# First attention of an encoder trunk: each turn of probabilities set directly ahead of later scores, dense steps dealt out anew

## Chip, cores and metric

One core of a Trainium2 chip runs the whole kernel in one launch. The metric is the device time of that launch in microseconds (us); a run's time is compared with runs of the kernel before. A difference of under 0.2% (2.7 us of 1348.9) can't be told from none.

## What is computed

Two layers on a sequence of 512 tokens of 1024 features, all in float32: layer 0 is windowed grouped-query attention with a sink logit, layer 1 a dilated attention in three groups, and each is followed by a SwiGLU block. The change touches layer 0's attention alone:

```python
def window_gqa_sink(h, w_qkv, w_out, sink):
    qkv = h @ w_qkv          # 16 query heads, 4 key/value heads of 64
    o, lse = banded_attention(q, k, v, slopes, 1, WINDOW_A, BLOCK_A)   # |t-s| <= 128, blocks of 128 queries
    o = o * jax.nn.sigmoid(lse - sink)
    return o.reshape(b, s, H_A * HEAD_DIM) @ w_out
```

In `banded_attention` the scores q·k get a bias from the distance, the probabilities are `exp(scores - max)` divided by their sum, and they weigh the values.

## The kernel before, in words

**Dense products.** The float32 operands of a dense product are split into a high and a low part (`split`, L115 on ScalarE for the high part `wh`, L116 on VectorE for the low part `wl`), and three matmuls stand for one product (`mm3`, L144). A dense product of 128 output features for all 512 tokens is a *unit* of 8 steps; a step is 6 matmuls of 256 columns. Weights arrive by DMA in buffers of three, and the two splits of a unit are made when a generator of that unit is first asked for a step.

**Attention in pieces.** Layer 0's attention is cut into 16 attention units (key-head pair P, half h, query block b; the list `units`). Unit n has four heads, and these steps:

- two score steps, `scores(0)` and `scores(1)`, numbered 2n and 2n+1 here (scores 0 to 31). Each is four matmuls (L168) into two PSUM banks with the tag `sc`, of which there are two. On the outer blocks (b = 0 and 3) they have 256 columns, on the inner ones 384. What follows each, on other engines: VectorE adds the bias and takes the maximum of both banks (L436, one instruction for each bank, *the reduction*), makes the negative maximum (L440), ScalarE takes the exponential of each (L443), VectorE the reciprocal (L445), and GpSimd scales (L447, tile `pr`).
- two or three turns (L454): four TensorE transposes of a 128-wide stretch of `pr` into a bank with the tag `tp`, of which there are two, then a copy out to `pt`, on VectorE for the second stretch (L458), else on ScalarE (L460). Turns are numbered 0 to 39 through the program. A turn needs `pr` of all four heads, so the scaling behind both score steps.
- a share in one of four weighings (L467): `weigh_four` takes four units at once, 40 matmuls; it writes one bank `sc` and the bank `ov`, and ScalarE and VectorE split the outcome (`oh` L484, `ol` L485).

**Order.** TensorE's order is the program's own. VectorE, ScalarE, GpSimd and SyncE get theirs from the scheduler, and each then runs its queue strictly in turn. In the program, units run two ahead: between the turns of unit n stand the score steps of unit n+2, and *dense steps* of another list (`fill`: the rest of the values' product, queries and keys of the second head pairs, the first parts of the output product) fill the time in which VectorE, ScalarE and GpSimd work. How many dense steps unit n gets is `counts[n]`; `weave` divides them evenly over the entries of its list of steps. Before unit 0 the number of dense steps between the first score steps is in the call of `spread`. These are L529 to L543 of the main body. In all 86 dense steps are spent here.

So what TensorE can wait for in this stretch is: a bank `sc` that a reduction (L436) has not yet read, for scores and for a weighing; `pr` that GpSimd has not yet scaled, for a turn; a bank `tp` whose copy isn't done.

Of the kernel before, what the change touches and what calls it, by code (L numbers as in the profile page):

```python
# [79 lines left out]
def trunk(ctx, tc, xT, gains, lastg, sink, tabs, qsc, wunits, wv, outT, outR):  # L80
# [96 lines left out]
    def chain(*gens):  # L177
        for _, g in gens:
            yield from g

    def weave(main, fill, total):

        done = 0
        for i, step in enumerate(main):
            want = total * (i + 1) // len(main)
            spread([step, want - done], fill)
            done = want

    def spread(main, fill):

        for step in main:
            if callable(step):
                step()
            else:
                for _ in range(step):
                    next(fill)
# [173 lines left out]
    with tc.tile_pool(name="l0", bufs=2) as pool:  # L370
# [10 lines left out]
        def late(gen):  # L381
            for _ in gen:
                for item in list(pending):
                    item[0] -= 1
                    if item[0] < 0:
                        pending.remove(item)
                        item[1]()
                yield

        def k_unit(P, **kw):  # L390
            def done(ps):
                t = spool.tile([128, S], F32, name="tmp")
                nc.vector.tensor_tensor(t, ps, norm["rb"], op=OP.mult)
                qk["k", P] = [pool.tile([128, S], F32R, name=f"kt{a}") for a in range(2)]
                qk["kl", P] = [pool.tile([128, S], F32R, name=f"kl{a}") for a in range(2)]
                split_keys(t, qk["k", P], qk["kl", P])
            return unit(5 * P, xh, xl, "mm", done, **kw)

        def q_unit(P, i, **kw):
            def done(ps):  # L400
                t = spool.tile([128, S], F32, name="tmp")
                col = 4 * P + i
                nc.vector.scalar_tensor_tensor(t, ps, qs_sb[:, col:col + 1], norm["rb"], op0=OP.mult, op1=OP.mult)
                qk["q", P, i] = apart(pool, any(k[0] == "q" for k in qk), lambda: [
                    pool.tile([128, S], F32R, name=f"qt{a}", bufs=6) for a in range(2)])
                if col < 2:
                    split_queries(t, qk["q", P, i])
                else:
                    pending.append([2, lambda: split_queries(t, qk["q", P, i])])
            return unit(5 * P + 1 + i, xh, xl, "mm", done, **kw)  # L410
# [63 lines left out]
        def weigh_four(n):  # L474

            for m, tag in ((n, "sc"), (n + 2, "ov")):
                ov = bank(tag, "ov")
                for k in range(2):
                    units[m + k][2](ov, k)
                P, h, b = m // 8, m // 4 % 2, m % 4  # L480
                own = slice(4 * P + 2 * h, 4 * P + 2 * h + 2)
                hi, lo = (t[:, own, 128 * b:128 * b + 256].rearrange("p i (b q) -> p b i q", b=2) for t in (oh, ol))
                src = ov.rearrange("p (b i q) -> p b i q", b=2, i=2)
                nc.scalar.activation(hi, src, AF.Copy)  # L484
                nc.vector.tensor_tensor(lo, src, hi.bitcast(F32), op=OP.subtract)  # L485
# [21 lines left out]
        def out_part(j, lo, hi, w={}, ahead=False):  # L507
            def gen():
                if lo == 0:
                    w[j] = load_unit(wunits[10 + j], (NK, 128))  # L510
                    if ahead:
                        yield
                    out_ps[j] = bank("mm")
                wh, wl = w[j]
                for c in range(lo, hi):
                    mm3(out_ps[j], wh[:, c], wl[:, c], oh[:, c, :], ol[:, c, :], c == 0, c == NK - 1)
                    if c == NK - 1:
                        residual(j, out_ps[j], 1)
                    yield
            return hi - lo, gen()  # L520
# [4 lines left out]
        fill = late(chain((16, early), q_unit(0, 2), q_unit(0, 3), k_unit(1),  # L525
                     *[q_unit(1, i) for i in range(4)],
                     *[out_part(j, 0, 4) for j in range(3)], *[out_part(j, 4, 6) for j in range(3)]))

        counts = [6, 7, 6, 5, 5, 5, 4, 4, 4, 4, 3, 2, 2, 2, 3, 2]  # L529
        units = [attention0(P, h, b) for P in range(2) for h in range(2) for b in range(4)]  # L530
        (s0, s1), (s2, s3) = units[0][0], units[1][0]
        spread([13, s0, 2, s1, 2, s2, 2, s3, 3], fill)
        for n, (_, rest, _) in enumerate(units):
            nexts = units[n + 2][0] if n + 2 < len(units) else []
            steps = []
            for k in range(len(rest)):
                steps += rest[k:k + 1]
                if k == 0 and n and n % 4 == 0:
                    steps.append(lambda: weigh_four(n - 4))
                steps += nexts[k:k + 1]  # L540
            if n == len(units) - 1:
                steps.append(lambda: weigh_four(n - 3))
            weave(steps, fill, counts[n])  # L543
# [588 lines left out]
    with tc.tile_pool(name="l1", bufs=2) as pool:  # L1132
# [41 lines left out]
        def behind(step):  # L1174
            def held():
                with tc.issue_after(newest(mybir.EngineType.Activation)):
                    step()
            return held
# [482 lines left out]
        def attention(p):  # L1661


            pts = {}

            def turn(ts):
                for t in ts:
                    pts[t] = turn_a(p, ts, t)

            def weigh():  # L1670
                early = p % 2 == 0 and p > 0
                if early:
                    scores_b(p, (0, 1))
                    scores_b(p, (2, 3))
                if p:
                    finish(p - 1)
                for t in range(4):
                    weigh_a(p, t, pts[t])
                if not early:
                    scores_b(p, (0, 1))  # L1680
                    scores_b(p, (2, 3))

            def turn_back():
                for cs in ((0, 1), (2, 3)):
                    st["pts", p, cs[0]] = turn_b(p, cs)
                merge_rows(p)

            low, high = (0, 1), (2, 3)
            return {"a01": lambda: scores_a(p, low), "a23": lambda: scores_a(p, high), "merge": lambda: merge(p),
                    "xa01": lambda: st["exps", p, low, "a"](), "xa23": lambda: st["exps", p, high, "a"](),  # L1690
                    "t01": lambda: turn(low), "t23": lambda: turn(high), "group": weigh,
                    "x0": lambda: st["exps", p, low](0), "x1": lambda: st["exps", p, low](1),
                    "x2": lambda: st["exps", p, high](2), "x3": lambda: st["exps", p, high](3),
                    "r01": lambda: st["rest", p, low](), "r23": lambda: st["rest", p, high](), "back": turn_back}
# [27 lines left out]
        def lined(made):  # L1722

            line, work = [], {}
            for n, gen, preps in made:
                for at, step in preps:
                    work.setdefault(max(len(line) + at, 0), []).append(step)
                line += [gen] * n
            for c, gen in enumerate(line):
                for step in work.pop(c, ()):  # L1730
                    step()
                next(gen, None)
                yield
# [31 lines left out]
        for _ in range(2):  # L1765
            both = pool.tile([128, 4, 256], F32, name="v1", bufs=3).rearrange("p (a b) f -> p a (b f)", a=2)
# [26 lines left out]
        counts = [sum(unit[0] for unit in units) for units in periods]  # L1793
        out_line = [plain_unit(j, lo, hi) for lo, hi in ((0, 6), (6, 7)) for j in range(3)]
        fill = lined([unit for units in periods for unit in units] + out_line)
# [28 lines left out]
        for p in range(8):  # L1824
# [6 lines left out]
            steps = attention(p)  # L1831
            steps = {name: behind(step) if f"{name}{p % 2}" in BEHIND else step for name, step in steps.items()}
# [98 lines left out]
```

## Time and profile before

| what | value |
|---|---|
| median of 3 runs | 1348.9 us (1347.6 to 1349.86) |
| the profiled execution's own time | 1346.77 us |
| its span | 1345.0 us |
| TensorE busy in the span | 1329.5 us (99%) |
| VectorE, ScalarE, GpSimd busy | 1071.2, 812.8, 286.0 us |
| granted TensorE clock | 1.00 |
| VectorE busy in 36 to 150 us | 80.08 of 114.00 us |
| ScalarE busy in 36 to 150 us | 76.72 of 114.00 us |

The first attention fills about 38 to 150 us of the span. In a row of the timeline stand the start, the duration, the engine, the line, the operation, out<-in, the shape and the count; behind it, in square brackets, how long the engine was idle before it and what ended that. Matmuls overlap one another, so a matmul's duration is not its cost: the cost is the distance from its start to the start of the next.

### The profile page before, as it was taken

What the parts mean: (1) busy time and instruction counts of PE and PEld (TensorE: products, weight loads), DVE (VectorE), ACT (ScalarE), POOL (GpSimd) and SP (SyncE); (2) the same over time, 40 slices, a digit from 0 to 9 for tenths busy, and PEclk for the clock granted to TensorE, in tenths of its full rate; (3) what the DMA queues carried; (4) which work ended last, traced back from release to release, by engine and by line L of the source; (5) the groups of instructions that cost most, each with busy time, mean ns of one, the idle gap of its engine ahead of it and who ended that gap; (6) DMA issues with size and microseconds to landing.
All of it is one profiled execution on the core that took longest, in us unless ns stands there. A gap on an engine that the chain in (4) does not pass through costs nothing.

```text
span 1345.0 us, 29672 instructions
## 1 busy us (share of the span) xinstructions
PE 1329.5 (99%) x11874; PEld 1309.5 (97%) x11874; DVE 1071.2 (80%) x1911; ACT 812.8 (60%) x1480; POOL 286.0 (21%) x388
## 2 busy tenths in 40 slices
PE   9999999999999999999999999999999999999998
PEld 8988999999999999999999999999999999999998
DVE  6776648877779999888888888888566887878995
ACT  6776534555555467667777667667454455555643
POOL 1233330111111001123314314313131011110203
PEclk9999999999999999999999999999999999999999
DMA  6210262688775547285556656655346388784822
GB/s 211 64 54 27 66 179 95 167 210 192 193 171 144 157 145 203 72 215 135 153 143 164 154 140 163 155 140 142 111 127 164 107 209 204 187 197 122 202 85 75
DMA packets 89914, 196.49 MB, mean 146 GB/s; under 512 B 11184, under 2 KB 17840, under 8 KB 89776
## 3 DMA queue, kind: packets, MB, share of 16 engines
q1 hardware_dynamic: 67072, 153.82, 36.2%
q0 software_dynamic: 22560, 40.52, 18.3%
q8 instruction: 93, 1.52, 0.5%
q14 instruction: 45, 0.37, 0.1%
q10 hardware_dynamic: 144, 0.26, 0.1%
HBM read 188.72 MB, written 5.84 MB: 145 GB/s over the span
## 4 chain that ended last, share of the span: by engine, by line
PE 85%; ACT 6%; DVE 4%; issue 2%; DMA 1%; SPq 0%; POOL 0%; DVEq 0%; ACTq 0%; POOLq 0%
PE mm L781 19%; PE sc L781 14%; PE mm L1337 13%; PE mm L144 12%; PE psv L144 9%; PE tp L144 6%; PE sc L144 2%; PE ov L467 1%; PE ov L144 1%; ACT pr L1587 1%; PE sc L1501 1%; ACT pr L443 1%; DVE wl L116 1%; PE ovb L1627 1%; PE tp L1529 1%
## 5 line engine op out<-in xcount | busy, mean ns | idle before, releaser
L737 POOL DMA_DIRECT2D w<-wunits x92 | 80.5, 916 | 446.5 <-DMA w<-wunits 187.6
L116 DVE TENSOR_TENSOR wl<-wraw,wh 128x1024 fp32r<-128x1024 f32 (+4 forms) x92 | 98.0, 1075 | 17.3 <-ACT wh L115 14.8
L115 ACT ACTIVATE wh<-wraw 128x1024 fp32r<-128x1024 f32 (+4 forms) x91 | 83.0, 928 | 45.2 <-PE mm L144 38.7
L781 PE MATMUL sc<-bh,wh 128*128 128x256 f32 x368 | 101.6, 276 | 0.0
L781 PE MATMUL mm<-bh,wl 128*128 128x256 f32 x368 | 101.6, 276 | 0.0
L781 PE MATMUL mm<-bh,h 128*128 128x256 f32 x368 | 101.6, 276 | 0.0
L781 PE MATMUL mm<-bh,wh 128*128 128x256 f32 x368 | 101.6, 276 | 0.0
L781 PE MATMUL sc<-bh,wl 128*128 128x256 f32 x368 | 101.6, 276 | 0.0
L781 PE MATMUL mm<-bl,wh 128*128 128x256 f32 x368 | 101.6, 276 | 0.0
L781 PE MATMUL sc<-bl,wh 128*128 128x256 f32 x368 | 101.6, 276 | 0.0
L781 PE MATMUL mm<-bl,h 128*128 128x256 f32 x368 | 101.6, 276 | 0.0
L781 PE MATMUL mm<-bh,l 128*128 128x256 f32 x368 | 101.6, 276 | 0.0
L144 PE MATMUL mm<-xh,wh 128*128 128x256 f32 x384 | 77.8, 284 | 0.0
L1337 PE MATMUL mm<-oh,slots 128*128 128x256 f32 x368 | 73.8, 285 | 2.4 <-ACT ssum L1352 2.0
L144 PE MATMUL mm<-xl,wh 128*128 128x256 f32 x384 | 75.5, 278 | 0.3 <-DVE xl L281 0.3
L144 PE MATMUL mm<-xh,wl 128*128 128x256 f32 x384 | 75.5, 278 | 0.2 <-DVE wl L116 0.2
L144 PE MATMUL psv<-wh,oh 128*128 128x256 f32 x256 | 71.2, 278 | 0.0
L144 PE MATMUL psv<-wl,oh 128*128 128x256 f32 x256 | 71.0, 277 | 0.2 <-DVE wl L116 0.2
L144 PE MATMUL psv<-wh,ol 128*128 128x256 f32 x256 | 70.9, 277 | 0.0
L781 PEld LDWEIGHTS mm<-bh,wh 128*128 128x128 f32 x368 | 69.1, 188 | 0.0
L781 PEld LDWEIGHTS sc<-bl,wh 128*128 128x128 f32 x368 | 69.1, 188 | 0.0
L781 PEld LDWEIGHTS mm<-bl,h 128*128 128x128 f32 x368 | 69.1, 188 | 0.0
(361 smaller groups left out, 5134.9 us busy)
## 6 DMA issues: line engine op xcount, KB each, us to landing
wraw<-wunits SPq DMA_DIRECT2D x118, 512.0 KB, 4.2
w<-wunits SPq DMA_DIRECT2D x207, 256.0 KB, 3.9
w<-wunits POOLq DMA_DIRECT2D x138, 256.0 KB, 6.3
wraw<-wv SPq DMA_DIRECT2D x21, 512.0 KB, 5.0
wraw<-wunits SPq DMA_DIRECT2D x16, 384.0 KB, 5.0
w<-wv SPq DMA_DIRECT2D x8, 512.0 KB, 4.3
w<-wv POOLq DMA_DIRECT2D x8, 512.0 KB, 7.3
wraw<-wunits SPq DMA_DIRECT2D x11, 256.0 KB, 3.2
```

Source lines behind the costliest of these rows:

```text
L115: nc.scalar.activation(out_h, src, AF.Copy)
L116: nc.vector.tensor_tensor(out_l, src, out_h.bitcast(F32), op=OP.subtract)
L144: nc.tensor.matmul(out[:, cols], a, b[:, cols], start=first and k == 0 and c == 0, stop=last and k == 2, skip_group_check=True)
L443: nc.scalar.activation(pr[:, e, :w + 1], pr[:, e, :w + 1], AF.Exp, bias=m[:, 1, e:e + 1], accum_out=m[:, 2, e:e + 1])
L467: nc.tensor.matmul(ov[64 * hf:64 * hf + 64, 256 * n:256 * n + 256], v0[:, k0 // 128 + kb, vs], st["pt", kb][:, 256 * hf:256 * hf + 256], s ...
L737: nc.gpsimd.dma_start(sums[:, 512 * k:512 * k + 512], v[:, 0:512], accum_op=OP.add)
L781: nc.tensor.matmul(out, a[:, j], b[:, j], start=first and j == 0 and i == 0, stop=j == 3 and i == 2, skip_group_check=True)
L1337: nc.tensor.matmul(out, a[:, j], b[:, j], start=first and j == 0 and i == 0, stop=j == 3 and i == 2, skip_group_check=True)
L1501: nc.tensor.matmul(out, qk["qs", p][a][:, 128 * t:128 * t + 128], kp[k], start=t == ts[0] and k == 0, stop=k == 1, skip_group_check=True)
L1529: nc.tensor.transpose(tp[:, (nb * a + kb) * 128:(nb * a + kb) * 128 + 128], st["pr", p, ts][:, a, o + 128 * kb:o + 128 * kb + 128], ident)
L1587: nc.scalar.activation(of(pr[:, a, :], c), of(pr[:, a, :], c), AF.Exp, bias=nm[:, c % 2, a:a + 1], accum_out=den[:, c % 2, a:a + 1])
L1627: nc.tensor.matmul(ov[rows, 128 * c:128 * c + 128], vals[p // 2, 1 + g][:, c, hv + 64 * a:hv + 64 * a + 64], pts[g][:, 256 * a + 128 * (c ...
```

## The change

Two things change, both in layer 0's attention. In the list of steps of unit n, the first turn and the first score step of unit n+2 become one entry, and so do the second turn and the second score step: no dense step stands between a turn and those scores any longer. Where a weighing belongs to unit n (n = 4, 8, 12), it now comes ahead of that unit's first turn, as an entry of its own. And the numbers of dense steps are others: `counts`, and the numbers between the first score steps. The total of dense steps stays 86.

```diff
-        counts = [6, 7, 6, 5, 5, 5, 4, 4, 4, 4, 3, 2, 2, 2, 3, 2]
+        counts = [6, 7, 6, 6, 4, 5, 3, 4, 4, 5, 1, 2, 2, 3, 3, 2]
         units = [attention0(P, h, b) for P in range(2) for h in range(2) for b in range(4)]
         (s0, s1), (s2, s3) = units[0][0], units[1][0]
-        spread([13, s0, 2, s1, 2, s2, 2, s3, 3], fill)
+        spread([13, s0, 2, s1, 1, s2, 4, s3, 3], fill)
         for n, (_, rest, _) in enumerate(units):
             nexts = units[n + 2][0] if n + 2 < len(units) else []
             steps = []
             for k in range(len(rest)):
-                steps += rest[k:k + 1]
+                both = rest[k:k + 1] if k else rest[:1] + nexts[:1]
                 if k == 0 and n and n % 4 == 0:
                     steps.append(lambda: weigh_four(n - 4))
-                steps += nexts[k:k + 1]
+                if k == 1:
+                    both = both + nexts[1:2]
+                steps.append(lambda both=both: [step() for step in both])
             if n == len(units) - 1:
                 steps.append(lambda: weigh_four(n - 3))
             weave(steps, fill, counts[n])
```

Three places show it. First TensorE around the second weighing. Before: scores 19 (four matmuls), one dense step, turn 20, the weighing, the next dense step.

```order
L168 MATMUL sc<-kt_873,qt_1176 128x384
L168 MATMUL sc<-kl_875,qt_1176 128x384
L168 MATMUL sc<-kt_874,qt_1177 128x384
L168 MATMUL sc<-kl_876,qt_1177 128x384
L144 MATMUL mm<-xh,wh 128x256 x2
L144 MATMUL mm<-xl,wh 128x256 x2
L144 MATMUL mm<-xh,wl 128x256 x2
L454 MATMUL tp<-ident,pr 128x128 x4
L467 MATMUL ov<-pt,v_101 64x256 x20
```

Of the change, the same place: turn 19, scores 19, two dense steps, the weighing.

```order
L454 MATMUL tp<-ident,pr 128x128 x4
L168 MATMUL sc<-kt_866,qt_1169 128x384
L168 MATMUL sc<-kl_868,qt_1169 128x384
L168 MATMUL sc<-kt_867,qt_1170 128x384
L168 MATMUL sc<-kl_869,qt_1170 128x384
L144 MATMUL mm<-xh,wh 128x256 x2
L144 MATMUL mm<-xl,wh 128x256 x2
L144 MATMUL mm<-xh,wl 128x256 x2
L144 MATMUL mm<-xh,wh 128x256 x2
L144 MATMUL mm<-xl,wh 128x256 x2
L144 MATMUL mm<-xh,wl 128x256 x2
L467 MATMUL ov<-pt,v_101 64x256 x20
```

Turn 20 has moved behind the weighing, and a second dense step stands between scores 19 and the weighing.

Second, VectorE at that place. Before: the reciprocal of scores 17, the split of a weight (L116), the two reductions of scores 18, the two parts of a split of queries (L155) around the negative maximum, the copy of turn 19, the first reduction of scores 19.

```order
L445 RECIPROCAL mst<-mst 128x2
L116 TENSOR_TENSOR wl<-wraw,wh 128x1024
L436 ISA pr,mst<-sc,tab_102 128x384
L436 ISA mst 128x1
L436 ISA pr,mst<-sc,tab_102 128x384
L436 ISA mst 128x1
L155 TENSOR_TENSOR qt_1338<-tmp,qt_1338 64x512
L440 SCALAR_TENSOR_TENSOR mst<-mst,nsink 128x2
L155 TENSOR_TENSOR qt_1339<-tmp,qt_1339 64x512
L458 COPY pt<-tp 128x512
L436 ISA pr,mst<-sc,tab_102 128x384
```

Of the change: the second reduction of scores 18, the same query splits and copy, both reductions of scores 19, the reciprocal of scores 18, and only then the split of the weight.

```order
L436 ISA pr,mst<-sc,tab_102 128x384
L436 ISA mst 128x1
L155 TENSOR_TENSOR qt_1338<-tmp,qt_1338 64x512
L440 SCALAR_TENSOR_TENSOR mst<-mst,nsink 128x2
L155 TENSOR_TENSOR qt_1339<-tmp,qt_1339 64x512
L458 COPY pt<-tp 128x512
L436 ISA pr,mst<-sc,tab_102 128x384
L436 ISA mst 128x1
L436 ISA pr,mst<-sc,tab_102 128x384
L436 ISA mst 128x1
L445 RECIPROCAL mst<-mst 128x2
L116 TENSOR_TENSOR wl<-wraw,wh 128x1024
```

The split of the weight has gone from ahead of scores 18 to behind scores 19.

Third, TensorE at unit 10. Before: scores 24, a dense step, turn 26, scores 25.

```order
L168 MATMUL sc<-kt_873,qt_1338 128x256
L168 MATMUL sc<-kl_875,qt_1338 128x256
L168 MATMUL sc<-kt_874,qt_1339 128x256
L168 MATMUL sc<-kl_876,qt_1339 128x256
L144 MATMUL mm<-oh,wh 128x256 x2
L144 MATMUL mm<-ol,wh 128x256 x2
L144 MATMUL mm<-oh,wl 128x256 x2
L454 MATMUL tp<-ident,pr 128x128 x4
L168 MATMUL sc<-kt_873,qt_1519 128x256
```

Of the change, from turn 25 to turn 27, with no dense step in it:

```order
L454 MATMUL tp<-ident,pr 128x128 x4
L168 MATMUL sc<-kt_866,qt_1338 128x256
L168 MATMUL sc<-kl_868,qt_1338 128x256
L168 MATMUL sc<-kt_867,qt_1339 128x256
L168 MATMUL sc<-kl_869,qt_1339 128x256
L454 MATMUL tp<-ident,pr 128x128 x4
L168 MATMUL sc<-kt_866,qt_1519 128x256
L168 MATMUL sc<-kl_868,qt_1519 128x256
L168 MATMUL sc<-kt_867,qt_1520 128x256
L168 MATMUL sc<-kl_869,qt_1520 128x256
L454 MATMUL tp<-ident,pr 128x128 x4
```

Between scores 24 and 25 only turn 26 is left. The four engines' instructions are the same in number and kind before and after, SyncE's order is the same, and outside the first attention no engine's order differs.

## The prediction

> **What bounds the kernel now.** I read the page first, then busy time by stretches, the waits of the first attention (36 to 150 us), and last the timeline of TensorE and VectorE there. The page:
>
> ```profile
> span 1345.0 us, 29672 instructions
> PE 1329.5 (99%) x11874; PEld 1309.5 (97%) x11874; DVE 1071.2 (80%) x1911; ACT 812.8 (60%) x1480; POOL 286.0 (21%) x388
> ```
>
> TensorE is busy nearly all the span, so only time that it loses can be won. Busy time by stretches, where the count of matmuls is in brackets:
>
> ```profile
> 100.00:125.00 25.00, 23.67 (x193) 21.43 (x193) 18.59 (x62) 16.29 (x44) 10.33 (x24) 1.00 0.14 43
> 225.00:250.00 25.00, 25.00 (x223) 25.00 (x222) 19.34 (x23) 12.80 (x17) 0.00 (x0) 1.00 0.35 107
> ```
>
> Within the first attention TensorE idles a little (23.67 of 25 us); in the dense block behind it, it doesn't. Both run at the full clock, 1.00. The waits there name the cause:
>
> ```profile
> PEld sc L168 <- DVE mst L436: 3.0, 8, 1.0
> ```
>
> Scores wait eight times for a reduction that has not yet read their bank. VectorE isn't out of capacity (18.59 of 25 us busy); its queue is at times in a bad order. To size each loss I need what a thing costs undisturbed. Scores 18, a dense step; then turn 15 with scores 16 directly behind it; then turn 30 with a weighing:
>
> ```profile
> 96.05 0.33 PE L168 MATMUL sc<-kt,qt 128*128 128x384 f32 x1
> ...
> 96.74 0.39 PE L144 MATMUL mm<-xh,wh 128*128 128x256 f32 x2
> ...
> 97.43 0.60 PE L454 MATMUL tp<-ident,pr 128*128 128x128 f32 x4
> ...
> 89.92 0.60 PE L454 MATMUL tp<-ident,pr 128*128 128x128 f32 x4
> 90.28 0.37 PE L168 MATMUL sc<-kt,qt 128*128 128x256 f32 x1
> ...
> 90.83 0.39 PE L144 MATMUL mm<-xh,wh 128*128 128x256 f32 x2
> ...
> 125.71 0.60 PE L454 MATMUL tp<-ident,pr 128*128 128x128 f32 x4
> 126.24 0.44 PE L467 MATMUL ov<-pt,v 128*64 128x256 f32 x2
> ```
>
> From start to start: scores of 384 columns 96.74 - 96.05 = 0.69, a dense step 97.43 - 96.74 = 0.69 (its thirds 0.23), a turn 0.36, a turn and scores of 256 together 90.83 - 89.92 = 0.91, a turn ahead of a weighing 0.53. Scores of 256 take two thirds of 0.69, 0.46. A turn directly ahead of scores thus costs TensorE nothing by itself (0.91 against 0.36 + 0.46 and the 0.09 that whatever follows a turn pays). The pairing is neutral; what counts is when banks come free.
>
> **What it removes.** The places where TensorE loses time, in order: ahead of and in scores 9, scores 11, scores 19, the second weighing, scores 24, scores 29, turn 35.
>
> ```profile
> 63.83 0.39 PE L144 MATMUL mm<-xh,wl 128*128 128x256 f32 x2
> 64.32 0.38 PE L168 MATMUL sc<-kt,qt 128*128 128x256 f32 x1
> ...
> 65.01 0.40 PE L144 MATMUL mm<-xh,wh 128*128 128x256 f32 x2
> ...
> 70.95 0.39 PE L144 MATMUL mm<-xh,wl 128*128 128x256 f32 x2
> 71.43 0.44 PE L168 MATMUL sc<-kt,qt 128*128 128x384 f32 x1
> ...
> 72.36 0.28 PE L144 MATMUL mm<-xh,wh 128*128 128x256 f32 x1
> ...
> 98.35 0.39 PE L144 MATMUL mm<-xh,wl 128*128 128x256 f32 x2
> 99.55 0.45 PE L168 MATMUL sc<-kt,qt 128*128 128x384 f32 x1 [0.81 <-DVE mst L436]
> ...
> 100.48 0.39 PE L144 MATMUL mm<-xh,wh 128*128 128x256 f32 x2
> ...
> 101.17 0.60 PE L454 MATMUL tp<-ident,pr 128*128 128x128 f32 x4
> 102.85 0.44 PE L467 MATMUL ov<-pt,v 128*64 128x256 f32 x2 [1.08 <-DVE mst L436]
> ...
> 117.01 0.60 PE L454 MATMUL tp<-ident,pr 128*128 128x128 f32 x4
> ...
> 118.55 0.28 PE L144 MATMUL mm<-oh,wh 128*128 128x256 f32 x1
> ...
> 132.19 0.60 PE L454 MATMUL tp<-ident,pr 128*128 128x128 f32 x4
> ...
> 133.61 0.39 PE L144 MATMUL mm<-oh,wh 128*128 128x256 f32 x2
> ...
> 137.94 1.16 PE L454 MATMUL tp<-ident,pr 128*128 128x128 f32 x4
> 138.85 0.36 PE L144 MATMUL mm<-oh,wh 128*128 128x256 f32 x1
> ```
>
> - Scores 9: due at 63.83 + 0.23 = 64.06, begun at 64.32 (0.26); then 0.69 long where 256 columns take 0.46 (0.23). Scores that had to wait run slower by about 0.23 besides. Together 0.49.
> - Scores 11: due at 71.18, begun at 71.43 (0.25), 0.93 instead of 0.69 (0.24): 0.49.
> - Scores 19: due at 98.58, begun at 99.55 (0.97), and 0.93 instead of 0.69 (0.24): 1.21.
> - Second weighing: 102.85 - 101.17 = 1.68 against 0.53: 1.15.
> - Turn 25 and scores 24: 118.55 - 117.01 = 1.54 against 0.91: 0.63.
> - Turn 31 and scores 29: 133.61 - 132.19 = 1.42 against 0.91 + 0.23 for the wider scores: 0.28.
> - Turn 35: 138.85 - 137.94 = 0.91 against 0.36: 0.55, a wait for GpSimd's scaling.
>
> The sum is 4.80 us, the most that the change can win; what scores 1 lose, below, stays, since both orders begin alike. Why the largest two go, VectorE shows:
>
> ```profile
> 97.79 1.23 DVE L116 TENSOR_TENSOR wl<-wraw,wh 128x1024 fp32r<-128x1024 f32 x1 [1.26 <-ACT wh L115]
> 98.94 0.55 DVE L436 CUSTOM_DVE_ANT_0 pr<-sc,tab 128x384 f32<-128x384 f32 x1
> ...
> 102.23 0.56 DVE L436 CUSTOM_DVE_ANT_0 pr<-sc,tab 128x384 f32<-128x384 f32 x1
> ```
>
> Scores 18 are done about 96.7, but in VectorE's queue a weight split stands ahead of their reduction; it idles 1.26 us for ScalarE's part and then works 1.23, so the reduction begins at 98.94. That delays scores 19 by 0.97, and the reduction of scores 19, at 102.23, delays the weighing. In the changed order the split stands behind both reductions of scores 19. Nothing else in that queue waits for ScalarE that long, and two dense steps instead of one and a turn stand ahead of the weighing. The others go by spacing, counted in the changed order: between scores 7 and 8 stand five dense steps instead of four (the reductions of 8, for which scores 9 waited, come up earlier beside them), between 10 and 11 three instead of two, between 23 and 24 four instead of two; scores 29 no longer meet the output split of the third weighing (L485) in front of their bank, since turn 30 now follows that weighing; and by turn 35 the reductions have caught up by some 0.6 us. I walked every score step, turn and weighing of the changed order through in this manner, each engine's queue in its order with the durations of before. All seven come out at zero. The margins are 0.1 to 0.7 us, so not each will.
>
> **What it adds.** Ahead of scores 2 stands one dense step where there were two:
>
> ```profile
> 40.25 0.38 PE L168 MATMUL sc<-kt,qt 128*128 128x256 f32 x1
> ...
> 41.66 0.42 DVE L436 CUSTOM_DVE_ANT_0 pr<-sc,tab 128x256 f32<-128x256 f32 x1
> ```
>
> Scores 1, begun at 40.25 late and slowed as scores 9 are (0.69), end at 40.94; a dense step later, at 41.63, scores 2 are due. The first bank is read from 41.66 to 42.08, in a part of VectorE's queue that is the same in both orders, so they begin at about 42.13: 0.50 lost, and 0.24 for the slow run, 0.74. This is the surest term. The dense step that is missing there follows later; it is moved, not spared.
>
> Scores 25 follow scores 24 with turn 26 alone between: due 0.46 + 0.36 = 0.82 us behind their start. From below it costs nothing, if VectorE is idle when scores 24 end; from above it costs 1.21, as scores 19 did. VectorE isn't idle: ahead of that reduction stand a query split and the reciprocal of scores 23, which waits for ScalarE. Nearest is scores 24 of before, which lost 0.63 with the same query splits ahead; I take 0.70.
>
> The second weighing: by my walk the reduction that frees its bank ends just when the weighing is due, 99.6 us on the clock of before. So it costs between zero and the 1.15 of today. What can shift it is a slowed query split:
>
> ```profile
> 90.26 1.40 DVE L116 TENSOR_TENSOR wl<-wraw,wh 128x1024 fp32r<-128x1024 f32 x1
> ...
> 90.11 1.90 POOL L447 TENSOR_SCALAR pr<-pr,mst 128x256 f32<-128x256 f32 x2 [0.28 <-DVE mst L445]
> L447 POOL TENSOR_SCALAR pr<-pr,mst 128x256 f32<-128x256 f32 x32 | 15.9, 509 | 37.4 <-DVE mst L440 25.6 <-DVE mst L445 11.6
> ```
>
> Two scalings that met a weight split took 1.90 us instead of twice 0.51, and the split 1.40 instead of 1.23: 0.17 for VectorE. In the changed order GpSimd's scaling of scores 17 falls on the two query splits ahead of that reduction: 2 x 0.17, so I take 0.35. [...]
>
> No instruction is added or taken away, no DMA issue moves in its queue, and dense steps only change places: cost zero, hidden by nothing, since TensorE does the same work. What ScalarE and GpSimd do later or earlier stays beside TensorE as long as no bank is missed. Behind 150 us TensorE was full and stays so; what it wins is handed through to the end, as the weights there are asked for in the same order when their buffers come free.
>
> **The sum.** 0.74 + 0.70 + 0.35 - 4.80 = -3.0 us. The profiled execution took 1346.77 us with a span of 1345.0, so it becomes 1343.8 and 1342.0. It lay 2.1 us under the median of the runs shown, 1348.9; carried over, the forecast is 1345.9. Of what a measurement can tell, 0.2% or 2.7 us, this is just beyond.
>
> **Rivals.**
> - *Tight places slip.* Several margins are 0.1 to 0.3 us (the second and third weighing, scores 5, 17 and 31). Each one missed costs its lateness and the 0.24 of slowed scores, some 0.5. With three missed, 3 x 0.5 = 1.5 is left of the gain: 1347.4. For it speaks that VectorE's durations vary by 0.2 (1.23 and 1.40 above); against it, that its idle time in the stretch is a quarter.
> - *Slower: narrowed pairs wait for a VectorE queue.* At six places (scores 12 and 13, 14 and 15, 16 and 17, 20 and 21, 22 and 23, 24 and 25) two dense steps and a turn, or two dense steps, between a pair's scores have shrunk by one. Of 384-column scores the bank of the first is read about 1.2 us after their start (0.63 until the first two matmuls have ended and VectorE has begun, an estimate from 96.05 and 0.33, then 0.55) and wanted after 0.69 + 0.69 + 0.36 = 1.74. From 0.55 us of delay in the queue each pair waits. If a weight split or its like stands ahead at each, as at scores 19, six times 1.21 is lost, and 7.3 + 0.7 - 4.8 = +3.2: 1352.1. For it speaks scores 25; against it that in the changed order of VectorE only copies of turns and a scaling of queries stand there, and no weight split directly ahead of any of these reductions but those of scores 18 in the order before.
> - *It does nothing for the end.* What TensorE wins here it waits later, for weights of the next block: 1348.9. The windows speak against it: 223 matmuls in 25 us behind the attention, with the DMA engines busy a third (0.35).
>
> **How the numbers follow.** My forecast gets 0.55, tight places 0.35, slower 0.05, nothing 0.05. Likeliest is 1345.9. From above the gain is bounded by 4.80 - 0.74 = 4.1 with both unknown costs at zero, 1344.8; the runs spread by about 1 us around their median, so the low end is 1344.0. The other end takes in the slipped places, 1347.4, and the same 1 us: 1348.4. Faster by over 0.2% is under 1346.2, which is my forecast but not the slipped places: 0.55. Within 0.2% are those and the case that nothing comes of it: 0.40. Slower: 0.05.
>
> **What would show it.** The last weighing of before begins here:
>
> ```profile
> 143.62 0.65 PE L467 MATMUL ov<-pt,v 128*64 128x256 f32 x4
> ```
>
> In the changed profile: scores 19 and the second weighing without an idle time for a reduction; the weight split (L116) there behind the reductions; scores 2 begun about 0.5 us after they are due, scores 25 with a wait of some 0.5; the first attention's last weighing about 3 us earlier than 143.62, and every later stretch as full as before. I am wrong if scores 12 to 23 show new waits for L436, if turns wait for GpSimd (L447) in more than one place, or if the last weighing is early and the end isn't.

## The result, and the profile after

The changed kernel took 1344.76 us (median of 7 runs, 1341.92 to 1346.2), the kernel before 1347.6 beside it (7 runs): a ratio of 0.9976, 95% interval 0.9965 to 0.9986. It is faster by 0.24%, 3.2 us, with 1.9 to 4.7 inside the interval. One execution of a kernel below (new entries in units 6 to 8 only) took 4736.83 us and is left out of its ratio. The profiled execution of the change took 1343.19 us, before 1346.77. Its page:

```profile
span 1341.4 us, 29671 instructions
PE 1328.7 (99%) x11874; PEld 1311.3 (98%) x11874; DVE 1071.1 (80%) x1911; ACT 813.3 (61%) x1480; POOL 287.1 (21%) x388
```

The work is the same on every engine to within about 1 us (VectorE 1071.1 against 1071.2, GpSimd 287.1 against 286.0); the span is 3.6 shorter. The waits of the first attention, 36 to 150 us, with the time in total, the number and the longest (PEld is TensorE's loading of weights, which stands ahead of the matmul):

```profile
PEld sc L168 <- DVE mst L436: 1.3, 3, 0.6
PEld ov L467 <- DVE mst L436: 0.2, 1, 0.2
```

The second weighing's wait of before, in the same view:

```profile
PEld ov L467 <- DVE mst L436: 1.3, 1, 1.3
```

Eight waits of scores have become three (scores 1, 2 and 25), the second weighing's load waits 0.2 where it had waited 1.3, and no turn waits for GpSimd. By stretches, TensorE gains in the attention, and stands as full behind it as it did. In such a row stand the stretch and its length, the busy time and number of instructions of TensorE, its weight loads, VectorE, ScalarE and GpSimd, the granted clock, the DMA engines' busy share and GB/s:

```profile
100.00:125.00 25.00, 24.85 (x208) 21.99 (x206) 17.78 (x62) 17.66 (x48) 12.73 (x28) 1.00 0.13 43
225.00:250.00 25.00, 25.00 (x223) 25.00 (x223) 20.44 (x24) 12.96 (x17) 1.77 (x2) 1.00 0.37 115
```

208 matmuls stand where 193 stood, though not all of them the same ones, since the program is some 3 us further on. TensorE's timeline at the places of the prediction: scores 0 and 2; turn 19 with scores 19 and the second weighing; turns 25 to 27 around scores 24 and 25; the last weighing.

```profile
37.39 0.28 PE L168 MATMUL sc<-kt,qt 128*128 128x256 f32 x1
...
40.62 0.39 PE L144 MATMUL mm<-xh,wl 128*128 128x256 f32 x2
41.37 0.45 PE L168 MATMUL sc<-kt,qt 128*128 128x384 f32 x1 [0.36 <-DVE mst L436]
...
42.17 0.40 PE L144 MATMUL mm<-xh,wh 128*128 128x256 f32 x2
...
96.36 0.60 PE L454 MATMUL tp<-ident,pr 128*128 128x128 f32 x4
96.72 0.42 PE L168 MATMUL sc<-kt,qt 128*128 128x384 f32 x1
...
98.69 0.40 PE L144 MATMUL mm<-xh,wl 128*128 128x256 f32 x2
99.08 4.54 PE L467 MATMUL ov<-pt,v 128*64 128x256 f32 x40
...
114.45 0.60 PE L454 MATMUL tp<-ident,pr 128*128 128x128 f32 x4
...
115.36 0.60 PE L454 MATMUL tp<-ident,pr 128*128 128x128 f32 x4
116.12 0.39 PE L168 MATMUL sc<-kt,qt 128*128 128x256 f32 x1 [0.15 <-DVE mst L436]
...
116.81 0.60 PE L454 MATMUL tp<-ident,pr 128*128 128x128 f32 x4
...
139.16 0.40 PE L144 MATMUL mm<-oh,wl 128*128 128x256 f32 x2
139.49 4.54 PE L467 MATMUL ov<-pt,v 128*64 128x256 f32 x40
```

Scores 19 begin 0.36 behind their turn, as undisturbed ones do. Scores 2 are due at 40.62 + 0.23 = 40.85, begin at 41.37 and run 0.80 instead of 0.69: 0.63 lost. Turn 26 with scores 25 takes 116.81 - 115.36 = 1.45, turn 25 with scores 24 115.36 - 114.45 = 0.91: 0.54 lost. The second weighing begins 99.08 - 98.69 = 0.39 behind the last third of a dense step, the last weighing 0.33: 0.06 lost. VectorE there:

```profile
97.12 0.71 DVE L155 TENSOR_TENSOR qt<-tmp,qt 64x512 fp32r<-64x512 f32 x1
...
98.46 0.56 DVE L436 CUSTOM_DVE_ANT_0 pr<-sc,tab 128x384 f32<-128x384 f32 x1
...
98.94 0.55 DVE L436 CUSTOM_DVE_ANT_0 pr<-sc,tab 128x384 f32<-128x384 f32 x1
...
99.50 1.20 DVE L116 TENSOR_TENSOR wl<-wraw,wh 128x1024 fp32r<-128x1024 f32 x1
```

The weight split follows both reductions of scores 19, and its 1.26 of waiting for ScalarE is gone too. The reduction that frees the weighing's bank ends at 98.46 + 0.56 = 99.02, the moment at which the weighing is due.

The size of the gain is best read from the start of scores 0 to the start of the last weighing. For that, the start of scores 0 before (its last weighing began at 143.62):

```profile
38.19 0.28 PE L168 MATMUL sc<-kt,qt 128*128 128x256 f32 x1
```

Before 143.62 - 38.19 = 105.43 us, after 139.49 - 37.39 = 102.10: 3.33 less. This *stretch* is used below for every kernel; it leaves out the start of the program, which was 0.80 shorter in this execution, and what follows.

### The profile page after: what moved, and what is told of

The parts are those of the page before. It is cut to its first block, busy times and chain, and to the rows that moved or that the text cites. A ratio compares the mean times of both kernels' runs of the same rounds, so it can differ in the third digit from the quotient of the medians.

```text
span 1341.4 us, 29671 instructions
## 1 busy us (share of the span) xinstructions
PE 1328.7 (99%) x11874; PEld 1311.3 (98%) x11874; DVE 1071.1 (80%) x1911; ACT 813.3 (61%) x1480; POOL 287.1 (21%) x388
## 4 chain that ended last, share of the span: by engine, by line
PE 90%; ACT 4%; DVE 4%; issue 1%; DVEq 0%; POOL 0%; ACTq 0%; POOLq 0%
PE mm L783 18%; PE mm L144 15%; PE mm L1339 14%; PE sc L783 14%; PE psv L144 9%; PE tp L144 6%; PE sc L144 2%; PE ov L467 1%; PE ov L144 1%; PE sc L168 1%; PE ovb L1629 1%; PE tp L454 1%; PE sc L1503 1%; ACT pr L1589 1%; PE sc L1569 1%
## 5 line engine op out<-in xcount | busy, mean ns | idle before, releaser
L116 DVE TENSOR_TENSOR wl<-wraw,wh 128x1024 fp32r<-128x1024 f32 (+4 forms) x92 | 98.7, 1082 | 15.7 <-ACT wh L115 13.1
L783 PEld LDWEIGHTS mm<-bh,l 128*128 128x128 f32 x368 | 69.1, 188 | 0.0
```

Of the source, the lines that this page charges most:

```text
L116: nc.vector.tensor_tensor(out_l, src, out_h.bitcast(F32), op=OP.subtract)
L783: nc.tensor.matmul(out, a[:, j], b[:, j], start=first and j == 0 and i == 0, stop=j == 3 and i == 2, skip_group_check=True)
```

## The experiments

My theory, A: TensorE loses time only where a reduction comes too late for its bank; the new entries set the turns and scores, the new numbers of dense steps give each bank its time, and it takes both. Rivals: the new entries alone do it (B), the new numbers alone (C); later, that one place in the middle carries nearly all (D), that the weight split is not the cause at scores 19 (F), and that a wait removed in one place turns up at another (E). The summary, with the ratio to the kernel before (95% interval) and the stretch of the profiled execution:

| kernel | ratio | stretch, us |
|---|---|---|
| before | 1 | 105.43 |
| the change | 0.9976 (0.9965 to 0.9986) | 102.10 |
| new entries only | 0.9993 (0.9985 to 1.0002) | 104.42 |
| new numbers only | 1.0002 (0.9993 to 1.0011) | 105.85 |
| new entries in units 6 to 8 only | 0.9982 (0.9973 to 0.9991) | 104.31 |
| the change without these | 0.9976 (0.9967 to 0.9986) | 101.85 |
| before, one weight split on GpSimd | 1.0006 (0.9997 to 1.0015) | 107.24 |
| the change, a step more ahead of scores 2 | 0.9971 (0.9961 to 0.9981) | 102.19 |
| the change, room at scores 25 | 0.9964 (0.9952 to 0.9977) | 102.15 |
| both of these | 0.9967 (0.9954 to 0.9979) | 101.93 |
| the change again | 0.9973 (0.9964 to 0.9982) | 102.41 |
| the change, unit 14 with two steps | 0.9978 (0.9969 to 0.9986) | 101.97 |
| room at 25, unit 14 with three | 0.9983 (0.9975 to 0.9992) | 102.69 |
| room at scores 1, 2 and 25 | 0.9962 (0.9950 to 0.9975) | 101.88 |

**New entries only.** The numbers of before, with the change's list of steps:

```diff
-                steps += rest[k:k + 1]
+                both = rest[k:k + 1] if k else rest[:1] + nexts[:1]
...
+                steps.append(lambda both=both: [step() for step in both])
```

> The new entries (turn directly ahead of scores, weighing ahead of the first turn), with the old numbers of dense steps. A, waits for banks set by VectorE's queue: the losses at scores 9, 11, 19, 24, 29 and turn 35 go, scores 2 lose nothing; but in this queue the weight split stands ahead of scores 19's reduction, so the second weighing still waits some 1.3 us, and scores 31 follow scores 30 with a turn alone between and lose about 0.6. Together about 2.9 us faster than before (2 to 3.5). B, the pairing itself spares TensorE time: all of the change's gain, 3.3 us, without any wait at the weighing mattering. C, the numbers of dense steps make the gain: none, within 0.5 us of before.

The stretch shrinks by 1.0. The second weighing still waits, as A said (it loses 0.89, A had some 1.3), but the gain is a third of A's, since scores wait at places that I had not seen. The largest, VectorE and TensorE at scores 10:

```profile
66.47 1.56 DVE L162 TENSOR_TENSOR kl<-tmp,kt 64x512 fp32r<-64x512 f32 x2
68.07 0.42 DVE L436 CUSTOM_DVE_ANT_0 pr<-sc,tab 128x256 f32<-128x256 f32 x1
...
67.49 0.60 PE L454 MATMUL tp<-ident,pr 128*128 128x128 f32 x4
68.56 0.45 PE L168 MATMUL sc<-kt,qt 128*128 128x384 f32 x1 [0.47 <-DVE mst L436]
```

Scores 10 are due at 67.49 + 0.36 = 67.85 and begin at 68.56: two splits of keys stand ahead of the reduction of scores 9. Scores 6, 7 and 31 lose some 0.4 each besides. B is refuted: the interval leaves at most 2 us. Against C, no gain, speaks the profile, though the timed interval just holds 1.

**New numbers only.** The list of steps of before, with `counts` and `spread` of the change.

> The new numbers of dense steps, with the old entries. A: VectorE's queue gets worse. A weight split and two key splits stand ahead of scores 8's reductions, so scores 9 lose some 2 us; the first weighing waits 1 to 2 us behind a weight split and query splits, scores 23 lose 0.9, scores 7 0.5 to 0.8, scores 2 and 25 as in the change; scores 19 lose nothing and the second weighing 0.3. Together 1 to 4 us slower than before, about 2.5. B: no pairing, no gain, within 0.5 us of before plus scores 2, +0.6. C: the whole gain, 3.3 us faster.

Nothing is won (interval 0.9993 to 1.0011), so C is refuted; A's sign is borne out by the stretch, though only just (0.42 longer), and its size is not: scores 7 and 23, for which A had a loss, lose nothing, the first weighing loses 0.8 instead of 1 to 2, and scores 25 lose 1.1 where A had some 0.5. At scores 9, VectorE and TensorE:

```profile
63.42 1.23 DVE L116 TENSOR_TENSOR wl<-wraw,wh 128x1024 fp32r<-128x1024 f32 x1 [0.68 <-ACT wh L115]
64.56 1.40 DVE L162 TENSOR_TENSOR kl<-tmp,kt 64x512 fp32r<-64x512 f32 x2
65.99 0.42 DVE L436 CUSTOM_DVE_ANT_0 pr<-sc,tab 128x256 f32<-128x256 f32 x1
...
66.48 0.38 PE L168 MATMUL sc<-kt,qt 128*128 128x256 f32 x1 [1.25 <-DVE mst L436]
...
102.82 0.54 DVE L436 CUSTOM_DVE_ANT_0 pr<-sc,tab 128x384 f32<-128x384 f32 x1
103.28 1.37 DVE L116 TENSOR_TENSOR wl<-wraw,wh 128x1024 fp32r<-128x1024 f32 x1
```

A weight split and two key splits ahead of the reduction of scores 8 cost TensorE 1.25 us of idle time. The last two rows are the other place: with the new numbers alone the weight split already stands behind the last reduction of scores 19. Entries -1.0 and numbers +0.4 make -0.6; together they make -3.3. So the two parts depend on each other, as A has it.

**New entries in units 6 to 8 only**, around the second weighing, all else as before:

```diff
+                if n in (6, 7, 8):
+                    both = rest[k:k + 1] if k else rest[:1] + nexts[:1]
...
+                    continue
                 steps += rest[k:k + 1]
```

> The kernel before, with units 6, 7 and 8 alone in the new entries (the place of scores 18 and 19 and the second weighing); numbers of dense steps as before. A: scores 19 lose nothing (1.21 won), but here the weight split stands between the reductions of scores 18 and those of scores 19, so the weighing loses 1.2 to 1.4 as before, and scores 17 lose about 0.3: 0.5 to 1.2 us faster than before, about 0.9. Rival D, it is the room at this place that counts, two dense steps behind scores 19: both losses go, 2.4 us faster.

```profile
97.05 1.22 DVE L116 TENSOR_TENSOR wl<-wraw,wh 128x1024 fp32r<-128x1024 f32 x1
...
101.11 1.73 PE L467 MATMUL ov<-pt,v 128*64 128x256 f32 x14 [0.96 <-DVE mst L436]
```

The stretch is 1.12 shorter (A 0.9, D 2.4). Scores 19 begin on time, but the split now stands ahead of their reduction, and the weighing waits 0.96. Scores 17 lose 0.45 and scores 24, of which nothing was forecast, lose nothing. The timed gain (0.18%, 2.4 us; 0.9 to 2.7 in a thousand) is larger than the stretch and, taken alone, is what D had; the place speaks for A, since D had no wait at the weighing.

**The change without these**: the same condition turned round, `n not in (6, 7, 8)`, with the new numbers.

> The change, with units 6, 7 and 8 alone in the old entries (one dense step and a turn between scores 19 and the second weighing, as before), same numbers of dense steps. A: in this queue the weight split stands behind both reductions of scores 19, although the room is that of before; scores 19 lose nothing, the weighing only 0.2 to 0.4: about 3.0 us faster than before (2.6 to 3.3). D: the losses of scores 19 and the weighing come back, 2.4 us: 0.9 us faster than before.

A's -3.0 is borne out (timed 0.9976, 3.2 us; the stretch is 3.6 shorter, a little beyond A's 2.6 to 3.3) and D refuted. Scores 19 lose nothing here either, and the weighing loses 0.14 (A had 0.2 to 0.4). So the numbers of dense steps bring the weighing's time, and at scores 19 either part does.

**One weight split on GpSimd**, in the order of before: the split that stands ahead of the reductions of scores 18 there runs on the other engine.

```diff
-        nc.vector.tensor_tensor(out_l, src, out_h.bitcast(F32), op=OP.subtract)
+        (low or nc.vector).tensor_tensor(out_l, src, out_h.bitcast(F32), op=OP.subtract)
...
-                    w[j] = load_unit(wunits[10 + j], (NK, 128))
+                    w[j] = load_unit(wunits[10 + j], (NK, 128), low=nc.gpsimd if j == 1 else None)
```

> The kernel before, with one thing moved: the low part of one weight split (the one that stands ahead of the reductions of scores 18) is made on GpSimd instead of VectorE; entries and numbers of dense steps as before, TensorE's order untouched. A: scores 19 lose nothing more (1.21 won); the weighing still waits about as long as before, for the two query splits stand ahead of scores 19's reduction and ScalarE hands them over late: the stretch from scores 0 to the last weighing 1.2 us shorter, 104.2 instead of 105.43. If GpSimd holds the query splits up while it subtracts, down to 0.2 shorter. F, it isn't the weight split but TensorE's own order around turns and scores: no change, 105.4.

The timelines of GpSimd, VectorE and TensorE:

```profile
97.28 2.40 POOL L116 TENSOR_TENSOR wl<-wraw,wh 128x1024 fp32r<-128x1024 f32 x1 [0.29 <-ACT wh L115]
...
98.22 2.00 DVE L155 TENSOR_TENSOR qt<-tmp,qt 64x512 fp32r<-64x512 f32 x1 [1.10 <-ACT qt L154]
...
97.95 0.33 PE L168 MATMUL sc<-kt,qt 128*128 128x384 f32 x1
...
102.38 5.79 PE L467 MATMUL ov<-pt,v 128*64 128x256 f32 x36 [2.45 <-DVE mst L436]
```

With no split ahead of the reduction of scores 18, scores 19 begin at 97.95 with no idle time: that the split cost them their 1.21 is shown, against F. But while GpSimd subtracts (until 99.68) a query split takes 2.00, the next one, at 100.44, 0.69, and the weighing idles 2.45. The loss has moved, and grown: 1.21 won at scores 19, some 1.4 more lost ahead of the weighing, and 1.7 in it, which ran at a lower granted clock (0.77 and 0.66 in two stretches of 3 us, see the last section). Together that is the 1.8 by which the stretch is longer.

**A step more ahead of scores 2**, against the change:

```diff
-        spread([13, s0, 2, s1, 1, s2, 4, s3, 3], fill)
+        spread([13, s0, 2, s1, 2, s2, 3, s3, 3], fill)
```

> The change, with one dense step moved back ahead of scores 2 (two there, three ahead of scores 3). A: the 0.64 us that scores 2 lose goes and nothing takes its place: the stretch from scores 0 to the last weighing is 101.5 instead of 102.10, the time 3.9 us under before. E, VectorE's queue as a whole is the limit and a wait taken away comes back at later scores: 102.1, no gain.

The last third of the dense step ahead of scores 2, and the scores:

```profile
41.54 0.40 PE L144 MATMUL mm<-xh,wl 128*128 128x256 f32 x2
41.77 0.34 PE L168 MATMUL sc<-kt,qt 128*128 128x384 f32 x1
```

Scores 2 begin on time (41.54 + 0.23), and their first matmul takes 0.34 instead of 0.45: the 0.63 is gone there. Yet the stretch is no shorter: scores 1 lost 0.72 in this execution (0.49 in the change's), and scores 7 now lose 0.28. The first of these varies without any edit, as the change run again shows below; the second is a wait come back, so E is right in part.

**Room at scores 25**, and **both**:

```diff
-        counts = [6, 7, 6, 6, 4, 5, 3, 4, 4, 5, 1, 2, 2, 3, 3, 2]
+        counts = [6, 7, 6, 6, 4, 5, 3, 4, 4, 4, 3, 2, 2, 3, 2, 2]
```

> The change, with dense steps dealt out so that one stands between scores 24 and turn 26 (units 9, 10 and 14 get 4, 3 and 2 instead of 5, 1 and 3). A: the 0.5 us that scores 25 lose goes: 101.6 instead of 102.10 from scores 0 to the last weighing; turns 35 and 36 without a dense step between have their inputs in time. E: 102.1, the wait comes back at scores 26 to 31 or at the turns.

> The change with both, the dense step back ahead of scores 2 and the one at scores 25. A: the two add up, 101.0 instead of 102.10 from scores 0 to the last weighing, 4.4 us (0.3%) under before and 1.1 under the change. E: no better than the change.

Turn 26 and scores 25 with a dense step ahead of them:

```profile
116.05 0.60 PE L454 MATMUL tp<-ident,pr 128*128 128x128 f32 x4
116.41 0.36 PE L168 MATMUL sc<-kt,qt 128*128 128x256 f32 x1
```

Scores 25 begin 0.36 behind the turn: their wait goes, but for 0.11 in slow scores. In the stretch nothing shows of it, since scores 1 again lost 0.70. Both together come to 101.93 with scores 7 at 0.3 and scores 25 at 0.25; the 101.0 that A had is missed.

**The change again, and unit 14.** In the change's profile TensorE ran at a slower rhythm just behind the last weighing, at a granted clock of 1.00 and without idle time. One of three stretches of 10 us that read alike (150 to 180 us), with the number of matmuls in brackets, then the same of the kernel before:

```profile
160.00:170.00 10.00, 10.00 (x87) 1.00 0.30 97
```

```profile
160.00:170.00 10.00, 10.00 (x91) 1.00 0.38 127
```

87 matmuls against 91 in 10 us: 4 x 0.11 x 3 = 1.3 us in 30. Was that the price of the new order? Three kernels: the changed kernel itself; the change with units 13 and 14 at 4 and 2 dense steps; and the room at scores 25 with units 13 and 14 at 2 and 3.

> The changed kernel itself, nothing edited. Its profile had 87 matmuls in each 10 us behind the last weighing (150 to 180 us), where the kernel before has 90 to 91, at the same granted clock and with no idle time, worth about 1.2 us. Theory R, the slower rhythm belongs to this order of instructions: 87 again in all three stretches of 10 us, and the kernel at 0.997 to 0.998 of the one before. Rival T, it is a chance of one execution: 90 to 91 in at least one of the three stretches. The times of the stretch itself also tell how much varies from run to run without any edit: from the start of scores 0 to the start of the last weighing it took 102.1 us; the other kernels let me expect 101.6 to 102.4, most of it by what scores 1 lose (0.40 to 0.72).

> The change, with unit 13 at four dense steps (three) and unit 14 at two (three): one dense step behind turn 37 or so comes one place earlier, the other three engines' queues stay as they are. Theory U, the dense steps of unit 14 set the rhythm in which the dense block behind the last weighing begins: 90 to 91 matmuls in each 10 us from 150 to 180 us as in the run with room at scores 25, and the end about 1.2 us nearer, 0.996 to 0.997 of the kernel before. Rival V, it hangs on what stands earlier (scores 25 or unit 10): 87 matmuls still, 0.997 to 0.998. The stretch up to the last weighing 102.1 us by both.

> The change with two more dense steps in unit 10, taken from units 9 and 13, and unit 14 left at three. Against the run that took them from units 9 and 14, one dense step of unit 13 or 14 is elsewhere. Theory U (unit 14 sets the rhythm behind the last weighing): scores 25 lose at most 0.1 to 0.25, the stretch up to the last weighing is 101.6 us, and behind it 87 matmuls in each 10 us: 0.9965 to 0.9975 of the kernel before. Rival V (it hangs on unit 10): 90 to 91 matmuls, 0.996 to 0.997.

The changed kernel, run again:

```profile
160.00:170.00 10.00, 10.00 (x91) 1.00 0.32 102
```

The same instructions now run at 91 in all three. So the rhythm belongs to the execution and not to the order: T is right, R is refuted, and U and V fall with it (all three kernels had 90 to 91). The same pair shows what varies without any edit: the stretch 102.10 and 102.41, scores 1 losing 0.49 and 0.71. Differences of 0.3 us between stretches are no finding. Most of it is scores 1, which both orders leave alone: without their loss the two read 101.61 and 101.70, the kernel before 105.43 - 0.40 = 105.03, the step ahead of scores 2 and the room at scores 25 101.47 and 101.45. So each of these two won perhaps 0.2, and not the 0.5 or 0.6 that A had. The third kernel loses 0.4 at scores 31, as the new entries alone did; both give unit 13 two dense steps.

**Room at scores 1, 2 and 25**: the counts of the room at scores 25, and 3, 2 and 2 dense steps between the first scores.

> The numbers of the run with room at scores 25 (units 9, 10 and 14 changed), and between the first score steps 3, 2 and 2 dense steps where the change has 2, 1 and 4: scores 3 and all later ones stand where the change has them. Theory A (spacing decides: scores whose bank is read before they are due lose nothing, and the dense step that goes there is not lost): scores 1 are due 0.69 us later, behind the reading of their bank, scores 2 too, and with scores 25 no place of the stretch waits for L436: 102.15 - 0.70 - 0.64 = 100.8 us from scores 0 to the last weighing, against 105.4 before and 102.1 of the change, and 0.995 to 0.997 of the kernel before. Rival E (room given at one place moves the queue of VectorE and the wait turns up again): with these numbers a weight split goes ahead of the negative maximum of scores 3, which delays the turns and scores behind it; some 0.3 to 1.2 us come back at scores 4 to 9 as 0.3 did at scores 7 when scores 2 got their step back: 101.1 to 102.0 us.

TensorE at scores 3, then VectorE ahead of the reductions of scores 2:

```profile
43.81 0.40 PE L144 MATMUL mm<-xh,wl 128*128 128x256 f32 x2
44.20 0.44 PE L168 MATMUL sc<-kt,qt 128*128 128x384 f32 x1
...
43.52 0.17 DVE L445 RECIPROCAL mst<-mst 128x2 f32<-128x2 f32 x1 [1.62 <-ACT pr L443]
43.60 0.54 DVE L436 CUSTOM_DVE_ANT_0 pr<-sc,tab 128x384 f32<-128x384 f32 x1
```

Scores 1 and 2 lose nothing and scores 25 0.26. But the scheduler now sets a reciprocal ahead of the reductions of scores 2, and VectorE idles 1.62 us for ScalarE; the weight split that E named stands behind the reductions of scores 3 (at 47.21). Scores 3 lose 0.4, scores 5 0.3, scores 7 0.2. The stretch is 101.88, in E's range; since scores 1 lose nothing in it, the rest of it is no better than the change's 101.61. Its ratio, 0.9962, like the 0.9964 of the room at scores 25, is the best measured, but both intervals overlap that of the change: a faster version is possible and not shown.

## Why the prediction held, step by step

It forecast -3.0 us; the two timings of the changed kernel give 0.9976 and 0.9973, 3.2 and 3.6 us. The median came out at 1344.76 and not 1345.9 mainly because the base was read 1.3 too high: 1348.9 from three runs, 1347.6 from seven.

- *Removed, 4.80*: six of the seven losses read zero in the profile after, and the second weighing 0.06, which is counted below. Right.
- *Why the largest two go*: right for the change, but too simple. The split behind both reductions is the work of the new numbers; with the new entries alone it stands between the reductions of scores 18 and 19, which spares scores 19 and not the weighing. That the split was the cause at scores 19 is shown by moving it to GpSimd.
- *Scores 2*: 0.74 forecast, 0.63 measured; begun 0.52 late (0.50 forecast), slowed by 0.11 and not 0.24. Only one of the two halves was slow.
- *Scores 25*: 0.70 forecast, 0.54 measured, for the reason given: the reduction waits behind a query split and a reciprocal. Here a query split did run slow beside GpSimd (0.95 at 114.32, instead of 0.69), but the reciprocal behind it waited for ScalarE until 115.51 in any case.
- *The second weighing*: 0.35 forecast, 0.06 measured. The reduction ends on the moment, as walked. The term that failed is the slowed query split: the two ahead of that reduction, at 96.04 and 97.12, took 0.69 and 0.71. It was GpSimd that paid: its scalings at 95.64 took 1.43 instead of 0.93.
- *The sum*: 0.63 + 0.54 + 0.06 - 4.80 = -3.57; the stretch has -3.33. Of the difference, 0.09 is scores 1 (0.40 before, 0.49 after), which the prediction let stand, and varies from run to run; the rest I can't place.
- *What is won is handed through to the end*: right to within 0.5 us. From the start of the last weighing to the end of the span it took 1345.0 - 143.62 = 1201.4 before, and 1201.9 in both profiles of the change. In the first of these some 1.2 us went right behind the last weighing and half of it came back later; in the second nothing went there and 0.5 further on. The same part took 1201.0 and 1201.2 in two other profiles, with the new numbers only and with unit 14 at two steps, whose instructions there are the same, so the 0.5 is no more than executions differ by.
- *Rivals*: tight places did not slip in the change, but they are real: 0.2 to 0.7 comes back at scores 3, 5, 6, 7, 10 or 31 when an entry or a number is other than the change has it. Of the six narrowed pairs only scores 25 waits.

## What to carry to other kernels

In an order written out by hand, the interleaving and the fill between its steps are one choice: each alone won a third of the gain or nothing, and the pair all of it. Price such a change place by place, with the moment a bank is read against the moment it is wanted, and walk every queue again after each edit, since a scheduler may send a long instruction ahead of another reduction. When the stake is a few tenths of a microsecond, first run one kernel twice: what differs between its two profiles is the least by which a profile can be off.

## What the runs showed of the hardware

- *Two rhythms at one clock.* Dense float32 matmuls of 256 columns ran at 87 or at 91 in 10 us for some 30 us behind the last weighing, at a granted clock of 1.00, in two executions of the same kernel. What sets it is open; from 160 to 170 us five of the fourteen profiles had the slower one (87 or 88), the nine others 90 or 91.
- *A lower clock behind a short stop.* With the weight split on GpSimd, the weighing that had waited 2.45 us ran at a lower granted clock:

```profile
101.00:104.00 3.00, 1.62 (x10) 0.77 0.42 157
104.00:107.00 3.00, 3.00 (x22) 0.66 0.00 0
```

  3 x 0.23 + 3 x 0.34 = 1.7 us of clock are missing; the weighing took 6.22 us, 4.54 in the changed kernel. From 103.11 to 106.06 its weight loads stand 0.43 us apart in twos, and behind that 20 of them take 2.09 us, 0.21 for two: for some 3 us TensorE ran at about half its rate. Four other profiles lost as much near 520 us (a granted clock of 0.83 in 10 us with the new entries alone, with room at scores 1, 2 and 25, and with both a step more ahead of scores 2 and room at scores 25; 0.89 in 15 us with room at 25 and unit 14 at three), with TensorE idle there for 0.16 to 0.21 us; with the new entries alone (0.16) and with both (0.20) the timeline names a weight split. Nine others read 1.00 from 515 to 530 us, with 0.20 to 0.25 idle. With the new entries alone it reads:

```profile
520.00:530.00 10.00, 9.84 (x72) 0.83 1.05 236
```

  This is a part of why that profiled execution (1349.64 us) lies above its median (1346.49); the slower rhythm behind its last weighing is another, about 1.0 us by an estimate (88, 88 and 87 matmuls in 10 us, 90, 91 and 91 before: 9 x 0.11). The length of a stop alone doesn't decide: in the changed kernel one of 0.36 us (ahead of 41.37) was followed by a granted clock of 1.00 from 42 to 48 us. Sixteen matmuls of one column (L298), 1.7 us of them, stand shortly ahead of the stop near 520 us, in the changed kernel without the loss and with the new entries alone with it. So which stops cost this is not settled.
- *Who is slowed when VectorE and GpSimd work side by side.* With the weight split on GpSimd, a query split on VectorE took 2.00 us instead of 0.69: it began at 98.22, beside GpSimd's subtraction (97.28 to 99.68), and ended 0.54 behind that. In the changed order it is the other way round: GpSimd's scalings of 384 columns, beside the weight split at 99.50 and then without it:

```profile
99.67 2.04 POOL L447 TENSOR_SCALAR pr<-pr,mst 128x384 f32<-128x384 f32 x2 [1.80 <-DVE mst L445]
102.47 1.15 POOL L447 TENSOR_SCALAR pr<-pr,mst 128x384 f32<-128x384 f32 x2 [0.76 <-DVE mst L445]
```

  The scalings, begun 0.17 behind the split, took 0.89 longer, and the split its 1.20 (1.23 at 97.79 before). In both places the one that began later took longer; why is not shown.
